# Splitting the RMS norm between two phases of a diffusion backbone: the latent half beside the last products of the phase before, the context half behind the first products of the next

## The chip, the cores and the metric

The kernel runs on one core of a Trainium2 chip. A core has TensorE (PE in the profile; PEld is its weight load), VectorE (DVE), ScalarE (ACT), GpSimd (POOL) and SyncE (SP, which here issues the loads), each with a queue of its own that is worked off in order, and sixteen DMA engines. The metric is the time of one execution on the device, in microseconds; the median of several executions is what counts.

## What is computed

Two layers over 256 latent tokens and 256 context tokens of width 1024. Each layer is a half-step FFN, a token mixer and a second half-step FFN, and each of the three begins with an RMS norm whose scale and shift come from a modulation (adaLN) that differs between latent and context tokens:

```python
def rmsnorm(x, g):
    xf = x.astype(F32)
    y = xf * lax.rsqrt(jnp.mean(xf * xf, axis=-1, keepdims=True) + EPS)
    return (y * g.astype(F32)).astype(x.dtype)

def modulate(x, shift, scale):
    return x * (1 + scale) + shift

def ffn_half_step(h, g, shift, scale, gate, w1, w3, w2):
    u = modulate(rmsnorm(h, g), shift, scale)
    return h + 0.5 * gate * ((jax.nn.silu(u @ w1) * (u @ w3)) @ w2)
...
for l in range(DEPTH):
    h = ffn_half_step(h, ...)
    hc = ffn_half_step(hc, ...)
    u = modulate(rmsnorm(h, g_mix[l]), mod[:, :, 3], mod[:, :, 4])
    uc = modulate(rmsnorm(hc, g_mix[l]), mod_c[:, :, 3], mod_c[:, :, 4])
    y, yc = token_mixer(u, uc, ...)
    h = h + mod[:, :, 5] * y
    h = ffn_half_step(h, ...)
    if not last:
        hc = hc + mod_c[:, :, 5] * yc
        hc = ffn_half_step(hc, ...)
return h
```

The mixer holds attention, a pooling branch and a gated linear attention, joined by gates and one output projection. In the last layer only the latent tokens leave the mixer, so the last FFN has no context half.

## The kernel before

**Layout.** Channels lie on the 128 partitions, tokens along the free axis: columns 0 to 255 are latent (one stream, NL = 256), 256 to 511 context. The residual `h` has eight tiles of 128 channels (k or dc = 0 to 7). All products are made in three fp32r matmuls (`mm3`, lines 218 to 220): each operand is split into a high and a low part, `whi`/`wlo` for weights, `hi`/`lo` for activations and `uhi`/`ulo` for a norm's result; high by high, high by low, low by high. A weight is loaded as `raw` (four buffers), then split by ScalarE (line 184) and VectorE (line 196). Tiles of 128x512 come from one pool of 71 slots; PSUM has eight banks, one tile each.

**The norm** (`norm`). `square` adds h*h into `acc`, tile by tile, as `h` grows (ScalarE squares, VectorE adds, line 445). Per stream, `mean` sums `acc` over partitions with a matmul of ones into `ms` (line 461; in fp32 it is two instructions), and ScalarE makes `rstd` of it with Ln and Exp. `some` then makes each of the eight k: `ut` = h * scale * rstd (VectorE, line 468), `uhi` (ScalarE), `ulo` (VectorE, line 472). Before, one call makes mean and tiles of the latent stream, then mean and tiles of the context stream, and only then the phase's first products are written down.

**The phase behind it.** The first products of a phase (`dense` with `by_stream`) go through all k of the latent columns for four units of weights, twelve matmuls per k, and then through all k of the context columns. In the mixer two of the four units are q projections and two k/v ones.

**The phase ahead of it.** The FFN ends in `down([6, 7], ...)`: the last two output columns together, latent products of column 6, then of 7, then context products of 6, of 7. Behind each of the four goes a `grow` (line 498: h += gate * products, by VectorE) and a `square`. The mixer's first layer ends in `out([6, 7], True)`: `dense` by stream, in which columns 6 and 7 alternate at each k, and the four grows behind all of it.

**The rest around it.** The modulation vectors are made beside all this, in small steps that `adas(n)` takes from a generator: a step loads 512 KB of `w_ada` and adds it up on VectorE in four instructions (`adaacc`, line 356), or on PE (line 326); now and then PE sums up and transposes (lines 373 and 380). `ada_edge` puts one piece of it, on PE, ahead of the second FFN's first products. The instructions are not issued strictly as written: a scheduler orders each queue ahead of time, by the order of writing among what it reckons to be ready.

**Where norms stand.** With two streams, and not the first of all: into the mixer of layer 0, the second FFN of layer 0, the first FFN of layer 1, the mixer of layer 1. The last FFN's has one stream.

Of the kernel before, what the change touches and what calls it, by code (L numbers as in the profile page):

```python
# [15 lines left out]
P = 128  # L16
T = 512
NL = 256
D = 1024
KD = 8  # L20
# [3 lines left out]
DEPTH = 2  # L24
# [44 lines left out]
class Unit:  # L69


    def __init__(self, hi, lo, need):
        self.hi, self.lo, self.need = hi, lo, need
# [63 lines left out]
class Net:  # L137
    def __init__(self, nc, a, cst, msk, vecs, wa2, out, pools, w):
        self.nc, self.a, self.cst_in, self.msk_in, self.out, self.w = nc, a, cst, msk, out, w
        self.vec_in, self.wa2_in = vecs, wa2  # L140
        self.one, self.slots, self.small, self.psum = pools
        self.table, self.users, self.tc, self.evac, self.net = None, [], None, None, self
        self.pairs = {}
        self.have = set()
        self.after, self.accs, self.owed, self.on_pe, self.edge = iter(()), [], 0, False, []


# [304 lines left out]
    def norm(self, l, i, n):  # L452

        nc = self.nc
        streams = [slice(s * NL, (s + 1) * NL) for s in range(n // NL)]
        u = [(self.slot(F32R, "uhi"), self.slot(F32R, "ulo")) for k in range(KD)]
        rstd = self.slot(name="rstd")

        def mean(c):
            ms = self.ps("ms")  # L460
            nc.tensor.matmul(ms[:, c], self.mean, self.acc[:, c], start=True, stop=True)
            self.rstd_from(ms[:, c], rstd[:, c])

        def some(s, c, ks):
            for k in ks:
                assert {(l, i, k // 4), (l, i + 1, k // 4)} <= self.have
                t, (hi, lo) = self.half("ut"), u[k]
                nc.vector.scalar_tensor_tensor(out=t, in0=self.h[:, k, c], scalar=self.am[l][i + 1][:, k, s:s + 1],
                                               in1=rstd[:, c], op0=ALU.mult, op1=ALU.mult)
                b = self.mod[l][:, 8 * i + k, s:s + 1]  # L470
                self.act(out=hi[:, c], in_=t, func=AF.Identity, bias=b)
                nc.vector.scalar_tensor_tensor(out=lo[:, c], in0=t, scalar=b, in1=hi[:, c].bitcast(F32),  # L472
                                               op0=ALU.add, op1=ALU.subtract)

        if l == 0 and i == 0:
            for c in streams:
                mean(c)
            yield u
            for parts in (([0], range(1, 4)), (range(4, KD),)):
                for ks in parts:  # L480
                    for s, c in enumerate(streams):
                        some(s, c, ks)
                yield
        else:
            for s, c in enumerate(streams):
                mean(c)
                some(s, c, range(KD))
            yield u

    def grow(self, ps, k, l, i, c, last):  # L490

# [8 lines left out]
            if last:  # L500
                self.square(k, s)

    def dense(self, units, x, n, by_stream=False):

        out = [self.ps() for _ in units]
        n = n if isinstance(n, list) else [n] * len(units)
        nk = len(x)
        for s in range(2 if by_stream else 1):
            for k in range(nk):
                for unit, o, m in zip(units, out, n):  # L510
                    c = slice(s * NL, (s + 1) * NL) if by_stream else slice(0, m)
                    if c.stop <= m:
                        self.mm3(o[:, c], unit.block(k), (x[k][0][:, c], x[k][1][:, c]), k == 0, k == nk - 1)
        self.w.done(*units)
        return out

# [17 lines left out]
    def ffn(self, l, which, n, final):  # L534
        nc, a = self.nc, self.a
        phase = 2 * l + which - 1
        i = 0 if which == 1 else 6
        w1, w3, w2 = (a[f"ffn{which}_{x}"][l] for x in ("w1", "w3", "w2"))

        def unit(m):  # L540
            return [self.cols(w, 0, KD, m * P) for w in (w1, w3)]

        begin = l == 0 and which == 1
        ahead = 3 if begin else 2
        norm = self.norm(l, i, n)
        if begin:
            self.adas(5)
            u = next(norm)
            self.adas(5)
            self.w.room = ROOM_0  # L550
            first = unit(0)
            next(norm)
            self.w.room = ROOM_1
            first += unit(1) + unit(2)
        else:
            self.w.room = ROOM_FFN
            first = unit(0) + unit(1)
            u = next(norm)
            self.adas(ADA["pre"][phase])
            self.ada_edge((l, which))  # L560
        gate = self.am[l][i + 2]
# [2 lines left out]
        def tail(p1, p3):  # L564
            s = self.slot(name="silu")
            self.act(out=s[:, 0:n], in_=p1[:, 0:n], func=AF.Silu)
            nc.vector.tensor_tensor(out=s[:, 0:n], in0=s[:, 0:n], in1=p3[:, 0:n], op=ALU.mult)  # L567
            g.append(self.parts(s[:, 0:n], n))

        def up(m0, m1):  # L570
            for m in range(m0, m1):
                if m == 0:
                    if begin:
                        steps = [lambda: None] * S0 + [lambda: self.adas(S1)] * (S2 - 1) + [lambda: (self.adas(10 - (S2 - 1) * S1), next(norm))]
                        o = self.dense_first(first, u, steps)
                    else:
                        o = self.dense(first, u, n, n == T)
                    for j in range(ahead):
                        tail(*o[2 * j:2 * j + 2])
                    self.ada_edge_end()  # L580
                    if begin:
                        self.w.room = ROOM_FFN
                        self.setup_rest()
                elif m >= ahead:
                    tail(*self.dense(unit(m), u, n))
                    self.adas(ADA["up"][phase])

        def down(ks, half, spans):
            us = {k: (self.cols(w2, half * HALF, 6, k * P), self.cols(w2, half * HALF + 6, 5, k * P)) for k in ks}
            o = {k: self.ps() for k in ks}  # L590
            for c in spans:
                for k in ks:
                    for f in range(HALF):
                        self.mm3(o[k][:, c], us[k][f // 6].block(f % 6), (g[f][0][:, c], g[f][1][:, c]), f == 0, f == HALF - 1)
                    self.grow(o[k], k, l, i + 2, c, half == 1)
            for k in ks:
                self.w.done(*us[k])
            if len(ks) == 1:
                self.adas(ADA["down"][phase])

        if not final:
            for half in range(2):
                up(half * HALF, (half + 1) * HALF)
                for k in range(6):
                    down([k], half, [slice(0, T)])
                if half:
                    down([6, 7], half, [slice(0, NL), slice(NL, T)])
                else:
                    down([6], half, [slice(0, T)])
                    down([7], half, [slice(0, T)])  # L610
                g.clear()
            return
        up(0, 4)
        assert {(l, 8, 0), (l, 8, 1)} <= self.have

# [12 lines left out]
        for c in range(2):  # L628
# [7 lines left out]
            self.act(out=t, in_=ps, func=AF.Copy)  # L636
            gt.append(t)
        up(4, KF)
        o = [self.ps() for _ in range(4)]

# [9 lines left out]
        us = [self.cols(w2, f, 1, 0, D) for f in range(KF - LAST, KF)]  # L650
        for i in range(4):
            for f, unit_ in enumerate(us):
                product(i, KF - LAST + f, unit_)
            j, c = divmod(i, 2)
# [7 lines left out]
    def mixer(self, l):  # L662
        a = self.a
        full = l < DEPTH - 1
        n = T if full else NL
# [20 lines left out]
        units = [self.w.get(load, 1024, cut)] + [self.cols(w_in, 0, KD, c0) for c0 in (256, 0, P)]  # L686
        if l == 0:
# [1 line left out]
            self.nc.tensor.transpose(ps[:, 0:P], self.vrow, self.ident)  # L689
            self.nc.vector.tensor_copy(self.vec[1], ps[:, 0:P])  # L690
            self.vrow = None
        u = self.u = next(self.norm(l, 3, T))
        self.adas(ADA["premix"][l])
        self.ada_edge((l, 0))
        self.inp = self.dense(units, u, [T, T, n, n], True)
        self.ada_edge_end()
        self.gq, self.gk, self.gv = [], [], []
        self.oa, self.op, self.on, self.gr, self.gates, self.pz, self.m = [], [], [], [], {}, {}, {}
# [4 lines left out]
        while chains:  # L703
            for c in list(chains):
                k = next(c, None)
# [9 lines left out]
            pass  # L715
        m = [self.m[dc] for dc in range(KD)]

        def out(dcs, by_stream):
            us = [self.cols(a["w_out"][l], 0, KD, dc * P) for dc in dcs]
            o = self.dense(us, m, n, by_stream)  # L720
            for c in ([slice(0, NL), slice(NL, T)] if by_stream else [slice(0, n)]):
                for dc, p in zip(dcs, o):
                    self.grow(p, dc, l, 5, c, True)

        self.w.room = ROOM_FFN
        self.on_pe = False
        out([0, 1, 2, 3], False)
        out([4], False)
        out([5], False)
        if full:  # L730
            out([6, 7], True)
        else:
            out([6], False)
            out([7], False)

    def chain(self, *gens):
        for g in gens:
# [642 lines left out]
```

## Time and profile before

| | us |
|---|---|
| median of three runs | 2197.16 (2190.83 to 2200.12) |
| the profiled execution | 2196.74 |
| its span, first to last instruction | 2194.6 |
| mean granted clock of TensorE in it | 0.986 |
| bytes moved from and to memory | 290.43 MB, 132 GB/s in the mean |

The span leaves out what lies around the program, 2.1 us. A row of the timeline gives start and length in us, engine, line, operation, the tile written and those read, the shape, how many such instructions follow one another, and in brackets how long the engine had stood idle and what ended that. A row of the windows gives the stretch and its length, then busy time and count for PE, PEld, DVE, ACT and POOL, PE's granted clock, the DMA engines' busy share and GB/s. A row of a group ends in busy us and mean ns of one, then the idle time before them. A row of the waits gives the total, the times and the longest, in us.

### The profile page before, as it was taken

The page shows a single profiled execution, that of the slowest core. Times are in us where ns is not written, and L with a number is a line of the kernel's source. Part 1 is how long each engine was busy: PE and PEld are TensorE (multiplying, and loading weights), DVE is VectorE, ACT ScalarE, POOL GpSimd, SP SyncE. Part 2 cuts the span into 40 slices and gives each one's busy share as a digit, 9 for nine tenths or more (in the row PEclk, how much of TensorE's full clock was granted, in tenths as well). Part 3 has the DMA queues.
Part 4 walks back from the last instruction along what each step waited for, and adds up shares of the span by engine and source line. Part 5 has one row for each costly group of instructions (what it writes and reads, how often), then busy time and mean ns, then how long its engine had stood idle before and what let it go on. Part 6 is the DMA issues. An engine that isn't in the chain of part 4 may idle for free.

```text
span 2194.6 us, 30011 instructions
## 1 busy us (share of the span) xinstructions
PE 2120.3 (97%) x11524; PEld 1752.2 (80%) x11524; DVE 1348.6 (61%) x2657; ACT 893.9 (41%) x1807; POOL 5.2 (0%) x26
## 2 busy tenths in 40 slices
PE   7999999999999999999999999999999978999999
PEld 4878788876766777888788888887888867898997
DVE  4566477665365775556565585577545698666564
ACT  5223133354344445433233343222333656565452
POOL 0000000000000000000000000000000000000000
PEclk8999999999999999999999999999999999999999
DMA  9356355433432323435464454456442324466663
GB/s 313 98 151 195 101 169 147 110 96 110 121 96 58 85 70 89 127 106 151 142 174 139 128 155 117 144 164 176 127 109 73 94 65 112 116 183 173 185 192 132
DMA packets 431070, 290.43 MB, mean 132 GB/s; under 512 B 16464, under 2 KB 386768, under 8 KB 430928
## 3 DMA queue, kind: packets, MB, share of 16 engines
q1 hardware_dynamic: 430016, 287.09, 45.5%
q8 instruction: 90, 1.47, 0.3%
q10 hardware_dynamic: 912, 1.44, 0.2%
q14 instruction: 52, 0.43, 0.1%
HBM read 287.44 MB, written 1.05 MB: 131 GB/s over the span
## 4 chain that ended last, share of the span: by engine, by line
PE 81%; DVE 8%; DMA 5%; ACT 4%; issue 2%; ACTq 0%; DVEq 0%; SPq 0%
PE ps L218 19%; PE ps L220 19%; PE ps L219 19%; DMA raw<-in_ffn_w_dram 5%; PE fill L218 4%; PE fill L220 4%; PE fill L219 4%; DVE wlo L196 2%; PE ada L326 2%; ACT whi L184 1%; PE sc L1030 1%; DVE st L1223 1%; PE av L1066 1%; PE pt L1048 1%; DVE adaacc L356 1%
## 5 line engine op out<-in xcount | busy, mean ns | idle before, releaser
L196 DVE TENSOR_TENSOR wlo<-raw,whi 128x512 fp32r<-128x512 f32 (+3 forms) x912 | 530.3, 619 | 332.3 <-ACT whi L184 324.7
L184 ACT ACTIVATE whi<-raw 128x512 fp32r<-128x512 f32 (+3 forms) x912 | 472.1, 568 | 510.4 <-DMA raw<-in_ffn_w_dram 400.0
L218 PE MATMUL ps<-uhi,whi 128*128 128x512 f32 (+1 forms) x1620 | 564.2, 350 | 7.2 <-ACT uhi L184 5.1
L219 PE MATMUL ps<-ulo,whi 128*128 128x512 f32 (+1 forms) x1620 | 562.6, 348 | 0.0
L220 PE MATMUL ps<-uhi,wlo 128*128 128x512 f32 (+1 forms) x1620 | 562.2, 348 | 0.1
L218 PEld LDWEIGHTS ps<-uhi,whi 128*128 128x128 f32 x1620 | 308.0, 191 | 58.8 <-ACT uhi L184 8.9
L220 PEld LDWEIGHTS ps<-uhi,wlo 128*128 128x128 f32 x1620 | 309.0, 191 | 39.4 <-DVE wlo L196 1.5
L219 PEld LDWEIGHTS ps<-ulo,whi 128*128 128x128 f32 x1620 | 309.5, 191 | 38.2 <-DVE ulo L472 0.6
L218 PE MATMUL ps<-hi,whi 128*128 128x512 f32 (+1 forms) x738 | 271.1, 368 | 4.0 <-DVE h L498 2.5
L220 PE MATMUL ps<-hi,wlo 128*128 128x512 f32 (+1 forms) x738 | 270.5, 367 | 0.0
L219 PE MATMUL ps<-lo,whi 128*128 128x512 f32 (+1 forms) x738 | 270.3, 366 | 0.0
L356 DVE SCALAR_TENSOR_TENSOR adaacc<-raw,csil,adaacc 128x512 f32<-128x512 f32 x350 | 243.0, 743 | 5.2 <-DMA raw<-in_w_ada_dram 5.2
L218 PE MATMUL fill<-uhi,whi 128*128 128x512 f32 (+1 forms) x576 | 204.3, 355 | 0.0
L220 PE MATMUL fill<-uhi,wlo 128*128 128x512 f32 (+1 forms) x576 | 196.5, 341 | 0.0
L219 PE MATMUL fill<-ulo,whi 128*128 128x512 f32 (+1 forms) x576 | 195.9, 340 | 0.0
L567 DVE TENSOR_TENSOR silu<-silu,ps 128x512 f32<-128x512 f32 (+1 forms) x88 | 54.3, 617 | 194.6 <-PE ps L220 111.4
L218 PEld LDWEIGHTS ps<-hi,whi 128*128 128x128 f32 x738 | 139.9, 190 | 29.4 <-DVE h L498 2.7
L219 PEld LDWEIGHTS ps<-lo,whi 128*128 128x128 f32 x738 | 140.0, 190 | 22.6 <-DVE lo L196 0.2
L220 PEld LDWEIGHTS ps<-hi,wlo 128*128 128x128 f32 x738 | 139.9, 190 | 22.4
L184 ACT ACTIVATE silu<-ps 128x512 f32<-128x512 f32 (+1 forms) x88 | 47.5, 539 | 232.3 <-PE ps L220 232.2
L218 PEld LDWEIGHTS fill<-uhi,whi 128*128 128x128 f32 x576 | 109.4, 190 | 27.1 <-issue 10.9
L219 PEld LDWEIGHTS fill<-ulo,whi 128*128 128x128 f32 x576 | 109.5, 190 | 13.6 <-issue 2.4
(265 smaller groups left out, 2182.8 us busy)
## 6 DMA issues: line engine op xcount, KB each, us to landing
raw<-in_ffn_w_dram SPq DMA_DIRECT2D x198, 512.0 KB, 4.6
raw<-in_w_ada_dram SPq DMA_DIRECT2D x128, 512.0 KB, 3.9
raw<-in_w_in_dram SPq DMA_DIRECT2D x86, 512.0 KB, 4.8
raw<-in_ffn_w_dram SPq DMA_DIRECT2D x48, 384.0 KB, 4.1
raw<-in_ffn_w_dram SPq DMA_DIRECT2D x48, 320.0 KB, 3.3
raw<-in_w_branch_dram SPq DMA_DIRECT2D x48, 256.0 KB, 2.8
ada<-in_w_ada_dram SPq DMA_DIRECT2D x32, 256.0 KB, 5.4
raw<-in_w_out_dram SPq DMA_DIRECT2D x16, 512.0 KB, 4.9
```

The lines of the kernel that those rows point to most:

```text
L184: i = self.nc.scalar.activation(**k)
L196: self.nc.vector.tensor_tensor(out=lo, in0=src, in1=f32hi, op=ALU.subtract)
L218: mm(out, wh, xh, start=start, stop=False)
L219: mm(out, wh, xl, start=False, stop=False)
L220: mm(out, wl, xh, start=False, stop=stop)
L326: nc.tensor.matmul(ps[32 * g:32 * g + 32, :], self.csil[:, k, :], r[i], start=(k < 4), stop=(k >= 4))
L356: nc.vector.scalar_tensor_tensor(out=acc[s], in0=r[i], scalar=c, in1=acc[s], op0=ALU.mult, op1=ALU.add)
L567: nc.vector.tensor_tensor(out=s[:, 0:n], in0=s[:, 0:n], in1=p3[:, 0:n], op=ALU.mult)
L1030: nc.tensor.matmul(sc[:, 0:nk], q[h][:, tt * P:(tt + 1) * P], keys[h][:, k0:T], start=True, stop=True)
L1048: nc.tensor.transpose(pt[:, (2 * x + j) * P:(2 * x + j + 1) * P], ps_[j][:, (kt + x) * P:(kt + x + 1) * P], self.ident)
L1066: nc.tensor.matmul(av[0][64 * x:64 * x + 64, s * NL:(s + 1) * NL], v[2 * s + kt][:, (h + x) * 64:(h + x) * 64 + 64], pts[x][kt // 2][:, (k ...
L1223: nc.vector.scalar_tensor_tensor(out=to, in0=st[x // 4][o, x % 4, :], scalar=dec[o, hh, x:x + 1], in1=ds, op0=ALU.mult, op1=ALU.add)
```

## The change

The norm becomes a generator with more steps: it yields behind the mean of a stream and behind its tiles. `norm_ahead` makes the next phase's norm and runs its first step, the latent mean; it is called in the phase before, behind the context products of column 6 and ahead of their grow. `norm_go`, called where the whole norm was, makes the latent tiles. `dense` takes a call, `then`, that it makes behind the latent products of k = 0 and 1: the context mean and the context tiles. The steps of `adas` and `ada_edge` that stood behind the whole norm stand between its halves now. The mixer's last two output columns are made by `out_last`, one column after the other in each stream, with a grow behind each. The last FFN's norm, with one stream, keeps its order.

```diff
         else:
             for s, c in enumerate(streams):
                 mean(c)
+                yield u
                 some(s, c, range(KD))
-            yield u
+                yield u
+
+    def norm_ahead(self, l, i):
+
+        order = [(l, i) for l in range(DEPTH) for i in (0, 3, 6)]
+        self.ahead = self.norm(*order[order.index((l, i)) + 1], T)
+        next(self.ahead)
+
+    def norm_go(self, l, i, n):
+
+        norm = self.ahead
+        if norm is None:
+            norm = self.norm(l, i, n)
+            next(norm)
+        self.ahead = None
+        u = next(norm)
+        return u, lambda: [next(norm) for _ in range(2)] if n == T else None
...
                     if c.stop <= m:
                         self.mm3(o[:, c], unit.block(k), (x[k][0][:, c], x[k][1][:, c]), k == 0, k == nk - 1)
+                if then and s == 0 and k == 1:
+                    then()
...
-            u = next(norm)
+            u, rest = self.norm_go(l, i, n)
             self.adas(ADA["pre"][phase])
             self.ada_edge((l, which))
...
-                        o = self.dense(first, u, n, n == T)
+                        o = self.dense(first, u, n, n == T, rest)
...
                         self.mm3(o[k][:, c], us[k][f // 6].block(f % 6), (g[f][0][:, c], g[f][1][:, c]), f == 0, f == HALF - 1)
+                    if c.start and k == 6:
+                        self.norm_ahead(l, i)
                     self.grow(o[k], k, l, i + 2, c, half == 1)
...
-        u = self.u = next(self.norm(l, 3, T))
+        self.u, rest = self.norm_go(l, 3, T)
         self.adas(ADA["premix"][l])
         self.ada_edge((l, 0))
-        self.inp = self.dense(units, u, [T, T, n, n], True)
+        self.inp = self.dense(units, self.u, [T, T, n, n], True, rest)
...
+        def out_last(dcs):
+
+            us = [self.cols(a["w_out"][l], 0, KD, dc * P) for dc in dcs]
+            o = [self.ps() for _ in us]
+            for c in (slice(0, NL), slice(NL, T)):
+                for dc, unit, p in zip(dcs, us, o):
+                    for k in range(KD):
+                        self.mm3(p[:, c], unit.block(k), (m[k][0][:, c], m[k][1][:, c]), k == 0, k == KD - 1)
+                    if c.start and dc == dcs[0]:
+                        self.norm_ahead(l, 3)
                     self.grow(p, dc, l, 5, c, True)
+            self.w.done(*us)
...
         if full:
-            out([6, 7], True)
+            out_last([6, 7])
```

More of the change, by code (lines that the diff above doesn't have):

```diff
@@ L486, in norm @@
                 mean(c)
+                yield u
                 some(s, c, range(KD))
-            yield u
+                yield u
[8 more added lines that the diff above has]
+            next(norm)
+        self.ahead = None
+        u = next(norm)
+        return u, lambda: [next(norm) for _ in range(2)] if n == T else None
     def grow(self, ps, k, l, i, c, last):
@@ L501, in grow, with dense @@
                 self.square(k, s)
-    def dense(self, units, x, n, by_stream=False):
+    def dense(self, units, x, n, by_stream=False, then=None):
         out = [self.ps() for _ in units]
@@ L544, in ffn @@
         ahead = 3 if begin else 2
-        norm = self.norm(l, i, n)
         if begin:
+            norm = self.norm(l, i, n)
             self.adas(5)
@@ L716, in mixer, with out @@
         m = [self.m[dc] for dc in range(KD)]
-        def out(dcs, by_stream):
+        def out(dcs):
             us = [self.cols(a["w_out"][l], 0, KD, dc * P) for dc in dcs]
-            o = self.dense(us, m, n, by_stream)
-            for c in ([slice(0, NL), slice(NL, T)] if by_stream else [slice(0, n)]):
-                for dc, p in zip(dcs, o):
+            for dc, p in zip(dcs, self.dense(us, m, n)):
+                self.grow(p, dc, l, 5, slice(0, n), True)
+        def out_last(dcs):
[7 more added lines that the diff above has]
+                        self.norm_ahead(l, 3)
                     self.grow(p, dc, l, 5, c, True)
+            self.w.done(*us)
         self.w.room = ROOM_FFN
         self.on_pe = False
-        out([0, 1, 2, 3], False)
-        out([4], False)
-        out([5], False)
+        out([0, 1, 2, 3])
+        out([4])
+        out([5])
         if full:
-            out([6, 7], True)
+            out_last([6, 7])
         else:
-            out([6], False)
-            out([7], False)
+            out([6])
+            out([7])
     def chain(self, *gens):
```

## The prediction

> **What bounds the kernel now.** I read the page's first part, then the waits of TensorE behind 404 us, then PE's own timeline at the four places that the change touches.
>
> ```profile
> span 2194.6 us, 30011 instructions
> PE 2120.3 (97%) x11524; PEld 1752.2 (80%) x11524; DVE 1348.6 (61%) x2657; ACT 893.9 (41%) x1807; POOL 5.2 (0%) x26
> ...
> PE ms L461 <- DVE acc L445: 8.7, 6, 3.4
> ```
>
> PE holds 97% of the span, so a microsecond counts only where PE stands. The wait to look at is `ms` (the matmul that sums the squares) for `acc`: six times behind 404 us, 8.7 us. One of the six, the longest (3.4), belongs to the last FFN, whose norm has one stream and isn't split by the change. The others lie at four boundaries: A into the first mixer, B into the FFN behind it, C into layer 1, D into the second mixer. PE there, one row per run of instructions:
>
> ```profile
> 419.69 0.59 PE L461 MATMUL ms<-acc,cst 128*128 128x256 f32 x2
> 421.38 0.67 PE L461 MATMUL ms<-acc,cst 128*128 128x256 f32 x2 [1.09 <-DVE acc L445]
> 423.01 0.39 PE L218 MATMUL ps<-uhi,whi 128*128 128x256 f32 x1 [0.96 <-ACT uhi L184]
> ...
> 920.82 1.05 PE L326 MATMUL ada<-raw,csil 128*32 128x512 f32 x4
> 923.04 0.67 PE L461 MATMUL ms<-acc,cst 128*128 128x256 f32 x2 [1.17 <-DVE acc L445]
> 923.90 0.67 PE L461 MATMUL ms<-acc,cst 128*128 128x256 f32 x2 [0.19 <-DVE acc L445]
> 924.50 2.22 PE L326 MATMUL ada<-raw,csil 128*32 128x512 f32 x16
> 926.65 0.39 PE L218 MATMUL ps<-uhi,whi 128*128 128x256 f32 x1
> ...
> 1300.41 0.59 PE L461 MATMUL ms<-acc,cst 128*128 128x256 f32 x2
> 1302.42 0.67 PE L461 MATMUL ms<-acc,cst 128*128 128x256 f32 x2 [1.42 <-DVE acc L445]
> 1303.02 1.06 PE L373 MATMUL ada<-adaacc,cst 128*32 128x512 f32 x8
> 1304.02 0.39 PE L218 MATMUL ps<-uhi,whi 128*128 128x256 f32 x1
> ...
> 1680.57 0.59 PE L461 MATMUL ms<-acc,cst 128*128 128x256 f32 x2
> 1682.58 0.67 PE L461 MATMUL ms<-acc,cst 128*128 128x256 f32 x2 [1.42 <-DVE acc L445]
> 1683.43 0.39 PE L218 MATMUL ps<-uhi,whi 128*128 128x256 f32 x1 [0.17 <-ACT uhi L184]
> ```
>
> At A the latent mean is issued as the old phase's products end, the context mean stands 1.09 us for its `acc`, and the first product stands 0.96 us for the latent `uhi`. Both stops come from the order: PE issues both means before any product, though the first products need the latent half alone.
>
> **The change, part by part.** *What goes.* From the first non-product to the first product: A 423.01 - 419.69 = 3.32, B 926.65 - 920.82 = 5.83, C 1304.02 - 1300.41 = 3.61, D 1683.43 - 1680.57 = 2.86; together 15.62 us. Part of it is work that stays. The means' own length:
>
> ```profile
> L461 PE MATMUL ms<-acc,cst x22: 377/380/763, 22.5 to 1993.7; 128*128 128x256 f32 x22
> ```
>
> Two instructions of 0.38 last 0.59, so they start 0.21 apart, and a pair holds PE's stream for about 0.42: 0.85 per boundary, 3.4 for four. The ada matmuls stay: at B sixteen in 926.65 - 924.50 = 2.15 and four in a quarter of it, 0.54; at C eight in 1.00. Stays 7.09, goes 15.62 - 7.09 = 8.53.
>
> *A's slow clock goes too.* PE behind A, beside PE before it:
>
> ```profile
> 423.75:427.25 3.50, 3.50 (x19) 3.50 (x19) 3.50 (x10) 2.42 (x6) 0.00 (x0) 0.52 0.00 0
> ...
> 408.00:419.60 11.60, 11.60 (x99) 11.60 (x99) 2.63 (x6) 1.25 (x3) 0.00 (x0) 1.00 0.04 11
> ```
>
> At clock 1.00 a product of 256 columns takes 11.60/99 = 0.117 us; 19 of them would take 2.23, and took 3.50: 1.27 lost at clock 0.52. I count it as gone with the two stops (2.05 us) ahead of it. The other end is that it has another cause and stays: nothing gained, 2189.1 in place of the time below, a case inside the forecast's own range. The Trainium skill ("TensorE: Matmul & The Clock Gate", section "What's actually happening") has the clock halved after an idle window of about 3.4 us that runs free of the program. By that rule alone the stops at A are too short to cool PE, which speaks for the other end; the row, 0.52 right behind them, speaks against it, and I keep the term.
>
> *What is moved: the latent half.* It now starts when the latent `acc` is complete, amid the last products. At A, on DVE and in its groups from 415 to 447 us:
>
> ```profile
> 415.82 0.48 DVE L498 SCALAR_TENSOR_TENSOR h<-ps,am,h 128x256 f32<-128x256 f32 x1 [2.50 <-PE ps L220]
> 416.85 0.42 DVE L445 TENSOR_TENSOR acc<-acc,sq 128x256 f32<-128x256 f32 x1 [0.54 <-ACT sq L184]
> 419.78 0.48 DVE L498 SCALAR_TENSOR_TENSOR h<-ps,am,h 128x256 f32<-128x256 f32 x1 [2.51 <-PE ps L220]
> 420.18 0.28 DVE L690 COPY vec<-ps 128x128 f32<-128x128 f32 x1
> 420.81 0.42 DVE L445 TENSOR_TENSOR acc<-acc,sq 128x256 f32<-128x256 f32 x1 [0.35 <-ACT sq L184]
> 421.62 1.27 DVE L468 SCALAR_TENSOR_TENSOR ut<-h,am,rstd 128x256 f32<-128x256 f32 x3 [0.39 <-ACT rstd L184]
> ...
> L468 DVE SCALAR_TENSOR_TENSOR ut<-h,am,rstd 128x256 f32<-128x256 f32 x16 | 7.2, 479 | 0.4 <-ACT rstd L184 0.4
> L472 DVE SCALAR_TENSOR_TENSOR ulo<-ut,mod,uhi 128x256 fp32r<-128x256 f32 x16 | 7.2, 479 | 0.1
> ```
>
> Column 6's context products end at 415.8, column 7's at 419.7. The mean goes between them; mean to first `ut` took 421.62 - 419.69 = 1.93 and `ut` to first product 423.01 - 421.62 = 1.39, so the first latent tile is there at 415.8 + 3.32 = 419.1, before PE asks for it at 419.7 + 0.42 = 420.1. DVE makes a k in 2 x 0.45 = 0.9 us, PE eats one in 12 x 0.117 = 1.4. Hidden by DVE's idle 2.5 us; uncovered, it costs the 3.32 - 0.85 that I count as gain at A. That this early start happens although `vec` and the grow come first in the program rests on DVE's order already being one by readiness: the copy at 420.18, written behind the `acc` of 420.81, runs ahead of it.
>
> *The context half* follows 24 latent products. At A its mean is reached at 420.1 + 24 x 0.117 = 422.9, its `acc` is ready at 420.81 + 0.42 + 0.42 = 421.7: 1.2 us to spare. Its tiles must come by 420.1 + 96 x 0.117 + 0.42 = 431.8; DVE, free of the latent half by 425 (eight at 0.9), has several us in hand. So zero; behind the waiting mean all latent products queue, so without that cover it is a PE stop.
>
> *B's products in another order.* Still 96 of them, each column's latent ones now on their own. DVE stood before the four grows:
>
> ```profile
> 912.61 1.29 DVE L196 TENSOR_TENSOR wlo<-raw,whi 128x512 fp32r<-128x512 f32 x2
> 920.57 1.27 DVE L498 SCALAR_TENSOR_TENSOR h<-ps,mod,h 128x256 f32<-128x256 f32 x3 [6.66 <-PE ps L220]
> ```
>
> The latent grows can run in those 6.66 us. New there: column 6's context products write the bank that its latent grow reads, and wait for it, with column 7's 24 latent products (2.8 us) as cover.
>
> *C is the crowded one.*
>
> ```profile
> 1297.03 2.08 DVE L356 SCALAR_TENSOR_TENSOR adaacc<-raw,csil,adaacc 128x512 f32<-128x512 f32 x3 [0.69 <-DMA raw<-in_w_ada_dram]
> 1299.03 0.48 DVE L498 SCALAR_TENSOR_TENSOR h<-ps,am,h 128x256 f32<-128x256 f32 x1
> 1299.42 0.74 DVE L356 SCALAR_TENSOR_TENSOR adaacc<-raw,csil,adaacc 128x512 f32<-128x512 f32 x1
> ```
>
> DVE is taken until 1300.1, so the latent tiles come about when PE wants them, not before. Of C's 3.61 - 0.85 - 1.00 = 1.76 I take half, leaving out 0.9; ends: nothing and all.
>
> *At nothing:* the one ada step that now stands ahead of the context half at B (PE, counted) and C (four DVE instructions of 0.74, inside the hand above; its loads keep their order on SP). The table load for silu moves with the context half, under 96 latent products. The 17 tiles for `u` and `rstd` are claimed some 4 us sooner; if they had to wait for a slot, a stop like the one below, 4.0, is my upper end, nothing the lower, and I take nothing, since column 6's weights come free as they are claimed.
>
> **Sum:** 8.53 + 1.27 - 0.9 = 8.9 us. The profiled execution took 2196.74 (span 2194.6 and 2.1 around it), 0.4 under the median 2197.16: 2196.74 - 8.9 = **2187.8**.
>
> **The rivals.** One stop shows what a bad order on DVE costs:
>
> ```profile
> 1289.70 0.75 DVE L356 SCALAR_TENSOR_TENSOR adaacc<-raw,csil,adaacc 128x512 f32<-128x512 f32 x1 [0.68 <-DMA raw<-in_w_ada_dram]
> 1290.37 0.48 DVE L498 SCALAR_TENSOR_TENSOR h<-ps,am,h 128x256 f32<-128x256 f32 x1
> ...
> 1290.91 0.58 PE L218 MATMUL ps<-hi,whi 128*128 128x256 f32 x1 [2.51 <-DVE h L498]
> ...
> 1290.90:1294.30 3.40, 3.39 (x16) 3.39 (x17) 3.40 (x7) 1.57 (x3) 0.00 (x0) 0.50 0.69 180
> ...
> 1528.21 1.12 PE L380 MATMUL ada<-cst,adaev 128*128 128x128 f32 x4 [4.06 <-ACT adaev L184]
> ...
> 1528.20:1533.30 5.10, 5.09 (x14) 4.23 (x15) 4.72 (x11) 2.11 (x4) 0.00 (x0) 0.50 0.78 239
> ```
>
> Here a grow stands in DVE's queue behind an ada step that waits for its load; PE, which must not write that bank before, loses 2.51, and then 3.39 - 16 x 0.117 = 1.5 at clock 0.50: 4.0. The grow reads the bank's latent columns and the products write its context columns, and still they wait for one another. The Trainium skill ("PSUM — Partial Sum Buffer", section "PSUM bank collisions raise a hardware error") asks for just this guard, by bank and not by address; it speaks against B's new order, and the row agrees.
>
> 1. *Slower: a stop like that at each boundary.* The latent half's `ut` and `ulo` wait in DVE's queue ahead of the context grow, and the context mean stops PE inside the latent products. It decides from 1.2 us of delay at A. Price 4 x 4.0 - 8.9 = +7.1: 2203.8. For: C's queue; against: DVE's idle stretches at A, B, D. 0.12.
> 2. *It doesn't start early:* DVE and ACT keep the latent half behind the last grows, and PE saves only the context mean's stops, some 2 to 3 us: 2194. Against: the order by readiness. 0.13.
> 3. *More:* everything behind A is put in order anew, and stops that hang on order may fall out: 4.0 at 1290.91, and 4.06 + 5.10 x 0.5 = 6.6 at 1528.21. One: 2184 or 2181; both: 2177. New ones are as possible, at those prices. 0.20.
>
> **How the numbers follow.** Forecast 0.55, its own range 2185 to 2192 (C's 0.9 either way, A's 1.27, some cooling at B to D in other executions). The range 2179 to 2200 takes in rival 2 and most of 3, and leaves out both stops gone and rival 1. A measurement tells 0.5%, 11 us, from no change: faster means below 2186, which the lower end of the forecast (0.15) and rival 3 give: 0.35. Slower means above 2208, rival 1 with more stops: 0.05. Within: 0.60.
>
> **What would show it.** Right: no idle before `ms` at the four boundaries, one latent mean amid 256-column products, clock 1.00 behind A, first `ut` at A near 417.7, first product within 0.6 us of the last old one. Wrong: idle before the context mean, a product waiting for `h` at B, or new stops before L380.

## The result and the profile after

| | median, us | runs | ratio to before, 95% interval |
|---|---|---|---|
| before | 2196.69 (2190.83 to 2200.12) | 7 | |
| after | 2207.13 (2204.51 to 2211.47) | 7 | 1.005 (1.0036 to 1.0063) |

The changed kernel is 10.4 us slower, where 8.9 us less were forecast. Its line numbers are a little higher: L184 is now L185, L196 is L197, the three products L218 to L220 are L219 to L221, the sum of squares L445 is L446, the norm's L461, L468 and L472 are L462, L469 and L473, the grow L498 is L516, `ada`'s L373 is L374. The first lines of the page, then TensorE's waits behind 404 us (total, times, longest):

```profile
span 2205.3 us, 29982 instructions
...
PE 2124.8 (96%) x11524; PEld 1759.9 (80%) x11524; DVE 1349.1 (61%) x2657; ACT 893.3 (41%) x1807; POOL 5.2 (0%) x26
```

```profile
PE ps L219 <- ACT uhi L185: 8.0, 3, 3.8
...
PE ps L220 <- DVE ulo L473: 3.9, 2, 1.9
...
PE ms L462 <- DVE acc L446: 2.8, 1, 2.8
```

The change did what it says: of the six stops of `ms` for `acc`, five are gone, and the one left is the last FFN's. But the products behind the means now wait for what the norm makes, 8.0 + 3.9 us. TensorE's timeline at A, C and D in the kernel after:

```profile
413.70 0.59 PE L462 MATMUL ms<-acc,cst 128*128 128x256 f32 x2
...
418.08 0.27 PE L711 MATMUL ps<-cst,vrow 128*128 128x128 f32 x1
422.19 1.22 PE L219 MATMUL ps<-uhi,whi 128*128 128x256 f32 x4 [3.83 <-ACT uhi L185]
...
1302.04 1.06 PE L374 MATMUL ada<-adaacc,cst 128*32 128x512 f32 x8
1304.68 0.50 PE L219 MATMUL ps<-uhi,whi 128*128 128x256 f32 x2 [1.57 <-ACT uhi L185]
1307.11 0.58 PE L220 MATMUL ps<-ulo,whi 128*128 128x256 f32 x1 [1.93 <-DVE ulo L473]
...
1678.07 0.59 PE L462 MATMUL ms<-acc,cst 128*128 128x256 f32 x2
1685.17 0.50 PE L219 MATMUL ps<-uhi,whi 128*128 128x256 f32 x2 [2.56 <-ACT uhi L185]
1687.60 0.42 PE L220 MATMUL ps<-ulo,whi 128*128 128x256 f32 x1 [1.93 <-DVE ulo L473]
```

At A the latent mean is issued at 413.70, six microseconds earlier than before, as meant, and still the first product stands 3.83 us for `uhi`. What ScalarE does in between stands in its own timeline, after first and then before:

```profile
414.33 0.47 ACT L185 ACTIVATE rstd<-ms,eps 128x256 f32<-128x256 f32 x1 [3.39 <-PE ms L462]
...
415.01 0.41 ACT L185 ACTIVATE rstd<-rstd 128x256 f32<-128x256 f32 x1
415.32 3.22 ACT L185 ACTIVATE whi<-raw 128x512 fp32r<-128x512 f32 x6
...
419.22 1.13 ACT L185 ACTIVATE whi<-raw 128x512 fp32r<-128x512 f32 x2
421.63 0.51 ACT L185 ACTIVATE uhi<-ut,mod 128x256 fp32r<-128x256 f32 x1 [1.28 <-DVE ut L469]
...
1679.38 0.41 ACT L185 ACTIVATE rstd<-rstd 128x256 f32<-128x256 f32 x1
1679.68 3.22 ACT L185 ACTIVATE whi<-raw 128x512 fp32r<-128x512 f32 x6
```

```profile
393.29 1.16 ACT L184 ACTIVATE whi<-raw 128x512 fp32r<-128x512 f32 x2 [0.18 <-DMA raw<-in_w_in_dram]
395.64 1.15 ACT L184 ACTIVATE whi<-raw 128x512 fp32r<-128x512 f32 x2 [1.19 <-DMA raw<-in_w_in_dram]
397.43 1.15 ACT L184 ACTIVATE whi<-raw 128x512 fp32r<-128x512 f32 x2 [0.63 <-DMA raw<-in_w_in_dram]
```

Before, the next phase's weights are split as they land, some 20 us ahead of A. After, eight such splits run from 415.32 to 420.35, starting in the same breath in which `rstd` is done; at D (1679.38, 1679.68) it is the same. Their second half is on VectorE, ahead of `ut`:

```profile
415.97 2.50 DVE L197 TENSOR_TENSOR wlo<-raw,whi 128x512 fp32r<-128x512 f32 x4 [0.40 <-ACT whi L185]
418.38 0.48 DVE L516 SCALAR_TENSOR_TENSOR h<-ps,am,h 128x256 f32<-128x256 f32 x1
...
421.12 0.48 DVE L469 SCALAR_TENSOR_TENSOR ut<-h,am,rstd 128x256 f32<-128x256 f32 x1
```

The idle time on VectorE that was to hold the latent tiles holds weights instead, and `ut` comes at 421.12 in place of the 417.7 forecast. The load queue of the kernel after shows how long these weights were held back:

```profile
385.97 6.06 SPq L211 DMA_DIRECT2D raw<-in_w_in_dram  x4
417.29 0.37 SPq L310 DMA_DIRECT2D raw<-in_w_ada_dram  x1
```

Four loads, as many as there are `raw` buffers, are out by 392; then nothing is issued for 25 us, until the first splits free a buffer. Before, the next load went out at 395.28.

Where the microseconds are: the start of the same TensorE instruction in two profiles, subtracted, by stretches (times of before). The two right columns belong to experiments e5 and e8 below.

| stretch | after - before | e5 - before | e8 - before |
|---|---|---|---|
| up to A (419.6) | -1.5 | -1.6 | -2.3 |
| **A** (to 447.7) | +2.3 | -2.7 | -4.5 |
| to 902.9 | +0.1 | +2.0 | +0.6 |
| **B** (to 935.7) | +0.5 | -0.8 | -0.5 |
| to 1286.7 | +0.1 | -0.3 | +0.9 |
| **C** (to 1318.5) | +4.1 | -3.0 | -3.4 |
| to 1676.5 | -4.1 | +0.3 | -0.6 |
| **D** (to 1703.7) | +4.2 | -0.5 | -2.3 |
| mixer of layer 1 (to 1840.8) | +4.9 | +3.8 | +5.6 |
| the rest | +0.1 | +0.7 | +0.4 |
| together | +10.7 | -2.1 | -6.1 |

The four boundaries lose 11.1 us in place of the gain of 8.9. The mixer's +4.9, where the change has no instruction, is read in the last section. Read in the same way, the boundaries of e2, which has nothing of the change but the early request, differ from before by at most 0.2 us each; a stretch can also move without any cause in the kernel, as A does by its clock (last section).

### The profile page after: what moved, and what is told of

It reads as the page before. It is cut to its first block, busy times and chain, and to the rows that moved or that the text cites. A ratio compares the mean times of both kernels' runs of the same rounds, so it can differ in the third digit from the quotient of the medians.

```text
span 2205.3 us, 29982 instructions
## 1 busy us (share of the span) xinstructions
PE 2124.8 (96%) x11524; PEld 1759.9 (80%) x11524; DVE 1349.1 (61%) x2657; ACT 893.3 (41%) x1807; POOL 5.2 (0%) x26
## 4 chain that ended last, share of the span: by engine, by line
PE 80%; DVE 8%; DMA 7%; ACT 3%; issue 1%; SPq 0%; ACTq 0%; DVEq 0%
PE ps L219 19%; PE ps L220 19%; PE ps L221 19%; DMA raw<-in_ffn_w_dram 5%; PE fill L219 4%; PE fill L221 4%; PE fill L220 4%; DVE wlo L197 3%; PE sc L1063 1%; ACT whi L185 1%; PE ada L327 1%; DVE st L1256 1%; DMA ada<-in_w_ada_dram 1%; PE av L1099 1%; DVE adaacc L357 1%
## 5 line engine op out<-in xcount | busy, mean ns | idle before, releaser
L197 DVE TENSOR_TENSOR wlo<-raw,whi 128x512 fp32r<-128x512 f32 (+3 forms) x912 | 530.4, 620 | 327.4 <-ACT whi L185 317.4
L185 ACT ACTIVATE whi<-raw 128x512 fp32r<-128x512 f32 (+3 forms) x912 | 471.1, 567 | 498.3 <-DMA raw<-in_ffn_w_dram 396.8
L219 PE MATMUL ps<-uhi,whi 128*128 128x512 f32 (+1 forms) x1620 | 566.2, 351 | 12.3 <-ACT uhi L185 11.9
L220 PE MATMUL ps<-ulo,whi 128*128 128x512 f32 (+1 forms) x1620 | 563.9, 349 | 3.9 <-DVE ulo L473 3.9
L221 PE MATMUL ps<-uhi,wlo 128*128 128x512 f32 (+1 forms) x1620 | 563.7, 349 | 0.1
L219 PEld LDWEIGHTS ps<-uhi,whi 128*128 128x128 f32 x1620 | 309.4, 192 | 63.1 <-ACT uhi L185 15.2
L220 PEld LDWEIGHTS ps<-ulo,whi 128*128 128x128 f32 x1620 | 310.7, 192 | 42.1 <-DVE ulo L473 4.8
L221 PEld LDWEIGHTS ps<-uhi,wlo 128*128 128x128 f32 x1620 | 310.5, 192 | 40.5 <-issue 1.7
L219 PE MATMUL ps<-hi,whi 128*128 128x512 f32 (+1 forms) x738 | 271.9, 369 | 3.7 <-DVE h L516 2.2
L221 PE MATMUL ps<-hi,wlo 128*128 128x512 f32 (+1 forms) x738 | 270.4, 366 | 0.0
L220 PE MATMUL ps<-lo,whi 128*128 128x512 f32 (+1 forms) x738 | 270.2, 366 | 0.0
L219 PE MATMUL fill<-uhi,whi 128*128 128x512 f32 (+1 forms) x576 | 204.9, 356 | 0.0
L221 PE MATMUL fill<-uhi,wlo 128*128 128x512 f32 (+1 forms) x576 | 197.1, 342 | 0.0
L220 PE MATMUL fill<-ulo,whi 128*128 128x512 f32 (+1 forms) x576 | 196.5, 341 | 0.0
L219 PEld LDWEIGHTS ps<-hi,whi 128*128 128x128 f32 x738 | 139.7, 189 | 29.2 <-DVE h L516 2.4
L220 PEld LDWEIGHTS ps<-lo,whi 128*128 128x128 f32 x738 | 139.9, 190 | 22.6 <-DVE lo L197 0.2
L221 PEld LDWEIGHTS ps<-hi,wlo 128*128 128x128 f32 x738 | 139.8, 189 | 22.5
L185 ACT ACTIVATE silu<-ps 128x512 f32<-128x512 f32 (+1 forms) x88 | 47.5, 540 | 233.5 <-PE ps L221 233.5
L219 PEld LDWEIGHTS fill<-uhi,whi 128*128 128x128 f32 x576 | 110.0, 191 | 27.1 <-issue 11.5
L220 PEld LDWEIGHTS fill<-ulo,whi 128*128 128x128 f32 x576 | 110.1, 191 | 13.7 <-issue 2.4
```

Source lines behind the costliest of these rows:

```text
L185: i = self.nc.scalar.activation(**k)
L197: self.nc.vector.tensor_tensor(out=lo, in0=src, in1=f32hi, op=ALU.subtract)
L219: mm(out, wh, xh, start=start, stop=False)
L220: mm(out, wh, xl, start=False, stop=False)
L221: mm(out, wl, xh, start=False, stop=stop)
```

## The experiments

**The theory** at the start: the early claim of 17 slots holds back the weights that are fetched ahead, because the slots run out. **Rivals**: it isn't their number but the order in which slots are handed out; or the context half behind the first products, or the new `out_last`, costs it.

**e1: claim the sixteen tiles of `u` late**, on the kernel after; `rstd` stays early.

```diff
-        u = [(self.slot(F32R, "uhi"), self.slot(F32R, "ulo")) for k in range(KD)]
+        u = []
+        claim = lambda: u.extend((self.slot(F32R, "uhi"), self.slot(F32R, "ulo")) for k in range(KD))
...
                 mean(c)
                 yield u
+                if s == 0:
+                    claim()
                 some(s, c, range(KD))
```

> The changed kernel, but the 16 tiles of the norm's result are claimed where the latent tiles are made (behind the next phase's first weights), no longer where the latent mean is written. Slots theory: the early claim takes the slots that the next phase's first weights had, so that their splits fall between the phases; with the late claim the splits are back ahead of 410 us at the first boundary, PE's waits for uhi and ulo at the four boundaries are gone, and the time is 2186 to 2191 us. Order theory (the latent half comes late because the queues keep the order of writing, whatever the slots): as the changed kernel, 2207 us.

**e2: claim early, and nothing else**, on the kernel before: `u` and `rstd` are asked for where the change asks for them, but first written in the old place.

```diff
+    def claim(self):
+
+        self.early_u = [(self.slot(F32R, "uhi"), self.slot(F32R, "ulo")) for k in range(KD)], self.slot(name="rstd")
...
+                    if c.start and k == 6:
+                        self.claim()
                     self.grow(o[k], k, l, i + 2, c, half == 1)
...
             o = self.dense(us, m, n, by_stream)
+            if by_stream:
+                self.claim()
```

> The kernel before, with nothing moved but the claim: the 16 tiles and rstd are claimed at the place where the change puts its latent mean. Slots theory: slower than before by 4 to 12 us (2201 to 2209), with the splits of the first weights between the phases at A, C and D and PE waiting for uhi there. Order theory: as before, 2196.7 us within 2.

e1 took 2213.65 us (6 runs), ratio 1.0066 (1.0042 to 1.0091), outside both forecasts, and no better than the change itself (the intervals overlap); its splits still run in one block behind `rstd`:

```profile
415.32 0.41 ACT L185 ACTIVATE rstd<-rstd 128x256 f32<-128x256 f32 x1
415.63 3.23 ACT L185 ACTIVATE whi<-raw 128x512 fp32r<-128x512 f32 x6
```

e2 took 2196.57 (12 runs), ratio 0.9992 (0.9977 to 1.0008). So neither the sixteen slots nor the early request costs anything: the first theory falls. What e1 kept from the change, and e2 didn't have, is an `rstd` that is first *written* ahead of the next phase's weights.

**e3: the context half alone** behind the first products, on the kernel before; both halves otherwise where they were.

```diff
                 some(s, c, range(KD))
-            yield u
+                yield u
...
+                if then and s == 0 and k == 1:
+                    then()
...
-        self.inp = self.dense(units, u, [T, T, n, n], True)
+        self.inp = self.dense(units, u, [T, T, n, n], True, lambda: next(norm))
```

> The kernel before, with the context half alone moved behind the first latent products; the latent half and the claim stay. Both theories: the context mean's stops go (1.1 at A, 0.2 at B, 1.4 at C, 1.4 at D), 2191 to 2194 us. If it is the context half that costs (its mean stopping PE amid the latent products): slower than 2200 us, with idle before the context mean.

2203.68 us (12 runs), ratio 1.0018 (1.0004 to 1.0032): a miss of the 2191 to 2194, no gain and if anything a small loss, though no context mean stops TensorE. Its timeline of TensorE at A:

```profile
419.32 0.60 PE L461 MATMUL ms<-acc,cst 128*128 128x256 f32 x2
422.33 0.74 PE L218 MATMUL ps<-uhi,whi 128*128 128x256 f32 x4 [2.42 <-ACT uhi L184]
```

The stop for the context mean is gone, and one stop of 2.42 for the latent `uhi` stands there instead of 1.09 + 0.96. The context mean's stop had lain inside the latent chain (mean, `rstd`, `ut`, `uhi`; 422.33 - 419.32 = 3.0 us), which nothing shortens here. So the context half is worth nothing without the latent half.

**e4: the mixer's output columns one after the other**, on the kernel before (`out_last` as in the change, without `norm_ahead`).

```diff
+        def out_last(dcs):
...
+            for c in (slice(0, NL), slice(NL, T)):
+                for dc, unit, p in zip(dcs, us, o):
+                    for k in range(KD):
+                        self.mm3(p[:, c], unit.block(k), (m[k][0][:, c], m[k][1][:, c]), k == 0, k == KD - 1)
+                    self.grow(p, dc, l, 5, c, True)
```

> The kernel before, with the mixer's last two columns made one after the other and nothing else. Grows done earlier: up to 1.4 us less at B, 2195 to 2197 us. If the shared bank stops the products (a wait for h at B): up to 4 us more, 2200 us.

2196.83 us (12 runs), ratio 0.9991 (0.9976 to 1.0006): no difference. The kernel before, shared by e1 to e4, took 2199.58 (29 runs).

**e5: `rstd` in a buffer of its own**, on the kernel after. The buffer has the size of a slot, so the pool gives one up.

```diff
-NHALF, NSLOT, ROOM_FFN, ROOM_MIX, RAWS = 4, 71, 20, 20, 4
+NHALF, NSLOT, ROOM_FFN, ROOM_MIX, RAWS = 4, 70, 20, 20, 4
...
-        rstd = self.slot(name="rstd")
+        rstd = self.small.tile([P, T], F32, tag="rstd", name="rstd", bufs=1)
```

> The changed kernel with rstd in a buffer of its own, and the pool of slots cut from 71 to 70, so that the memory is the same. Claim-order theory: slots are given out in the order in which the tiles are first used in the program; rstd, whose first use waits for the latent squares, stands ahead of the next phase's first weights and holds back their slots, and with them their splits, raw buffers and loads. With rstd out of that pool the splits are back ahead of 410 us, PE's waits for uhi at A, C and D shrink to under 0.5 us, and the time is 2186 to 2192 us. Order theory (the latent half is late whatever holds the weights): 2205 to 2210 us, as the changed kernel.

**2193.69 us** (12 runs), ratio 0.998 (0.9967 to 0.9993): faster than both kernels, though above the 2186 to 2192 forecast. ScalarE's timeline has the splits back where they land:

```profile
392.53 1.16 ACT L185 ACTIVATE whi<-raw 128x512 fp32r<-128x512 f32 x2 [1.60 <-DMA raw<-in_w_in_dram]
```

**e6 and e7: the same test on another kernel.** e6 is the kernel after with only the latent mean early: context mean and context tiles are back ahead of the first products. e7 is e6 with e5's buffer.

```diff
         u = next(norm)
-        return u, lambda: [next(norm) for _ in range(2)] if n == T else None
+        if n == T:
+            next(norm), next(norm)
+        return u, None
```

> The changed kernel with the latent mean alone early: latent tiles, context mean and context tiles stand together where the whole norm stood, rstd in the slots. Claim-order theory: the weights are held back as in the changed kernel, 2203 to 2212 us, splits behind 412 us at A. If the latent tiles or the context half are what costs: about 2197 us or less.

> As the run with the mean alone early, but rstd in its own buffer and 70 slots. Claim-order theory: splits ahead of 410 us, the latent chain begun early, PE's stop at the boundary about the context mean's alone: 2189 to 2196 us. Other theories: as the run before it.

e6 took 2209.91 us (6 runs), ratio 1.0053 (1.0035 to 1.0071), as slow as the change; its splits run in one block from 414.37, behind an `rstd` of 414.06. e7 took 2198.8 (12 runs), ratio 1.0003 (0.9988 to 1.0018): its splits are out of that block, but it misses its 2189 to 2196. TensorE stands there for the context mean, 1.49 us at A, 0.81 at B, 1.81 at C and 1.79 at D. One tile moved out of the shared pool is worth 13.4 us after the change (2207.13 to 2193.69) and 11.1 here, and an early `rstd` alone is enough to cost it. Before, shared by e5 to e7, took 2196.98 (23 runs), close to the 2196.69 beside which 2207.13 was measured.

What remained: e5 gains 3 us and not 9, and its stops for `uhi` at A and D are not under 0.5. VectorE's timeline of e5 at A, then TensorE's:

```profile
415.09 0.42 DVE L446 TENSOR_TENSOR acc<-acc,sq 128x256 f32<-128x256 f32 x1 [0.76 <-ACT sq L185]
418.23 0.48 DVE L516 SCALAR_TENSOR_TENSOR h<-ps,am,h 128x256 f32<-128x256 f32 x1 [2.72 <-PE ps L221]
418.63 0.28 DVE L712 COPY vec<-ps 128x128 f32<-128x128 f32 x1
418.83 0.48 DVE L469 SCALAR_TENSOR_TENSOR ut<-h,am,rstd 128x256 f32<-128x256 f32 x1
```

```profile
418.03 0.27 PE L711 MATMUL ps<-cst,vrow 128*128 128x128 f32 x1
419.90 0.74 PE L219 MATMUL ps<-uhi,whi 128*128 128x256 f32 x4 [1.60 <-ACT uhi L185]
```

VectorE is idle for 2.72 us with `rstd` ready, and yet `ut` runs only behind the last grow. The same kind of order can do it: `ut` shares four buffers of one tag with `sq`, and the last context `sq` is written ahead of the first `ut` in the program. In the idle stretch none of the four holds an `sq` that is still wanted: the last one was read by 415.09 + 0.42, and the next is written at 418.75, behind that grow.

**e8: `ut` in buffers of its own** on top of e5 (four of them, so two slots fewer). **e9: the two slots fewer alone. e10: e5's buffer in the kernel before.**

```diff
-NHALF, NSLOT, ROOM_FFN, ROOM_MIX, RAWS = 4, 70, 20, 20, 4
+NHALF, NSLOT, ROOM_FFN, ROOM_MIX, RAWS = 4, 68, 20, 20, 4
...
-                t, (hi, lo) = self.half("ut"), u[k]
+                t, (hi, lo) = self.small.tile([P, NL], F32, tag="ut", name="ut", bufs=4), u[k]
```

> e5 with 68 slots in place of 70 and a tag of four buffers of its own for ut, which shared the four half-width buffers with sq. Theory: buffers of a tag are handed out in the order of first use in the program, so in e5 the first ut (418.83 us at A, behind the last grow at 418.23, though rstd is ready at 415.36 and DVE idle from 415.5 to 418.2) waits for the sq of column 7's context half. With its own buffers ut runs ahead of the last grow at A and D, PE's stops there (1.60 and 1.51 us for uhi in e5) shrink below 0.5, and C's 0.70 + 0.52 shrinks too: 3 to 4 us below e5, 2188 to 2191. Rival: ut waits for something else (DVE's order, u's slots): stops as in e5, and 2193 to 2196 as the two slots fewer allow.

> Control of e8: e5 with 68 slots in place of 70 and nothing else. If the count of slots matters little, as e1 and e2 let one think, the time of e5 within 3 us (2191 to 2197) with stops of about 1.5 us for uhi at A and D. If it matters, slower than e5 by more than 3 us, and e8 has to be read against this one.

> Control of e5: the kernel before with rstd in its own buffer and 70 slots. There rstd is first written right ahead of the next phase's products, behind the weights that are fetched ahead, so its place in the order of slots holds nothing back. Theory: the time of before within 2 us. Rival: a slot for rstd costs both kernels, and e5's gain is this and not the change: 3 us or more below before.

| | median, us (12 runs each) | ratio, 95% interval |
|---|---|---|
| before (29 runs) | 2197.4 | |
| e8 | **2190.77** | 0.9964 (0.9951 to 0.9977) |
| e9 | 2193.21 | 0.998 (0.9968 to 0.9991) |
| e10 | 2197.95 | 0.9996 (0.9984 to 1.0009) |

e8 at A, VectorE and then TensorE:

```profile
414.72 1.27 DVE L469 SCALAR_TENSOR_TENSOR ut<-h,am,rstd 128x256 f32<-128x256 f32 x3
...
417.88 0.48 DVE L516 SCALAR_TENSOR_TENSOR h<-ps,am,h 128x256 f32<-128x256 f32 x1
```

```profile
417.31 0.27 PE L711 MATMUL ps<-cst,vrow 128*128 128x128 f32 x1
417.34 0.36 PE L219 MATMUL ps<-uhi,whi 128*128 128x256 f32 x1
...
1292.87 1.06 PE L374 MATMUL ada<-adaacc,cst 128*32 128x512 f32 x8
1293.87 0.38 PE L219 MATMUL ps<-uhi,whi 128*128 128x256 f32 x1
1294.52 0.39 PE L220 MATMUL ps<-ulo,whi 128*128 128x256 f32 x1 [0.26 <-DVE ulo L473]
```

Three `ut` run ahead of the last grow, and the first product follows the last old one with no stop; at C 0.26 us is left there of 3.5, and TensorE's waits behind 404 us have no row for `uhi` any more and this one alone for `ulo`. Not all is gone at C: the latent mean stands 0.70 us there for `acc`, in e5, e8 and e9 alike. So `ut` did wait for `sq`'s buffers. In the medians e8 is 2.4 us below e9, with intervals that overlap; the stops gone at A and D (1.60 and 1.51 us in e5, the same again in e9) say more than these. e9 says that two slots don't matter, e10 that e5's buffer does nothing for the kernel before: what it removes came with the change. e5, e8 and e9 are below both kernels, and e8 is the lowest: 6.6 us under before in the medians, 5 to 11 by the interval.

## Why the prediction was wrong

The forecast was 2187.8 us in a range of 2179 to 2200; the kernel took 2207.13, slower than before instead of faster. By the prediction's own steps:

- **The step that failed** is under "At nothing": "The 17 tiles for `u` and `rstd` are claimed some 4 us sooner; ... I take nothing, since column 6's weights come free as they are claimed." It asked whether the slots suffice, and they do (e1, e2, e9). It didn't ask who stands behind them in line. Asking early costs nothing (e2), writing `rstd` early does (e6), and with a buffer of its own it doesn't (e5, e7); that fits tiles which share buffers getting them in the order of their first use in the program, and e8 is a second case. `rstd`, which can't be written before the latent squares are done, now stood ahead of the next phase's weights, so these waited from 392 to 415 us with their four loads in hand. The price was bounded at one stop of 4.0; it was paid at three boundaries (+2.3, +4.1, +4.2) and the gain didn't come.
- **The early start of the latent half** failed for the same kind of reason: "rests on DVE's order already being one by readiness". `ut` was ready by its data but not by its buffer. It cost e5 the 1.6 us at A and 1.5 at D that e8 has back.
- **The sum of the stops** came out near, partly by luck. In e8, where both orders are mended, the boundaries give 4.5 + 0.5 + 3.4 + 2.3 = 10.7 us, where 8.9 were forecast: 3.3 - 0.85 + 1.27 = 3.7 at A, 2.3 at B, 0.9 at C and 2.0 at D. Of A's 4.5, 1.5 is the clock of the next point. At B two terms counted as staying grew: the sixteen ada matmuls take 2.70 us and not 2.15, and the four others stand 0.54 for their load. Of C's 3.4, 3.2 lies ahead of the means, by the same reading of starts: the stop for `h` there, priced at 4.0 with its slow clock, shrank to 0.77 at full clock (first two rows below, timeline and window of e8). That isn't shown to be the change's, since e10, without any of it, has this stop at 1.10 and full clock too. The norm's own stops then give about 3.0 + 0.5 + 0.2 + 2.3 = 6.0 us in this profile, against 7.6 forecast without the clock; the medians of e8 and before differ by 6.6.

```profile
1283.40 0.39 PE L219 MATMUL ps<-hi,whi 128*128 128x256 f32 x1 [0.77 <-DVE h L516]
```

```profile
1283.40:1287.00 3.60, 3.60 (x30) 3.60 (x31) 3.60 (x7) 1.57 (x3) 0.00 (x0) 1.00 0.65 168
...
417.40:427.40 10.00, 10.00 (x84) 9.95 (x83) 9.85 (x26) 5.41 (x13) 0.00 (x0) 1.00 0.01 2
```

- **A's slow clock**, 1.27 of the sum, is not shown to go with the stops. The last row has 1.00 behind A where before had 0.52, but so have e4 and e10, which keep A's two stops as they were; e2, with the same stops, has 0.51. In e4 and e10 A is 1.5 us shorter than before by the clock alone. The term belongs at least in part to the one execution that was profiled, which is the other end that the prediction named.
- **Moving the context half** costs nothing, as forecast: e8's context mean stops TensorE at none of the four boundaries. e3 adds what the forecast hadn't said: without the early latent half it gains nothing either.
- **The rivals.** Rival 1 came nearest in its time (2203.8) and had the sign right, and stops came at three of its four boundaries; but that is luck, for its mechanism, `ut` and `ulo` in VectorE's queue ahead of the grow, isn't what happened. Rival 2 saw the latent half stay behind the last grows, which is what e5 does at A, with 2193.69 against its 2194; that is another kernel than the one forecast. Rival 3's stop at 1528.21 did get cheaper after the change, 3.02 us and no slow clock behind it, which is 3.4 of the table's -4.1. It need not be the change's: e5 and e8 don't have it, and e10, without the change, is 1.8 us shorter at this place.

## What to carry to other kernels

Before moving the first write of a tile forward, list what stands behind it in its pool: a tile that shares buffers with prefetched weights and is itself written late blocked the weights here, though the slots would have sufficed. Give such a tile, and any that shares a tag with work of another phase, a buffer of its own, and look in the profile for a block of splits that starts just as one small tile is done, and for a load queue that is silent for as long. A stop that was removed was worth nothing where the chain behind it stayed as long (e3). And before a slow clock in one profile is counted as gain, look whether other executions of the same code have it.

## What else the runs showed of the hardware

**The same stop cools TensorE in one execution and not in another.** In the mixer of layer 1 the code is the same before and after. One stop there, in the timeline and the window behind it, before and then after:

```profile
1803.67 0.46 PE L1240 MATMUL o<-Asum,gv 128*128 128x128 f32 x2 [2.35 <-DVE Asum L1236]
```

```profile
1803.67:1808.67 5.00, 5.00 (x43) 5.00 (x44) 3.99 (x11) 3.61 (x10) 0.00 (x0) 1.00 0.01 3
```

```profile
1810.93 0.77 PE L1273 MATMUL o<-Asum,gv 128*128 128x128 f32 x2 [2.36 <-DVE Asum L1269]
```

```profile
1810.93:1815.93 5.00, 5.00 (x23) 5.00 (x24) 3.99 (x11) 3.61 (x10) 0.00 (x0) 0.50 0.02 3
```

2.35 and 2.36 us of idleness, and then a granted clock of 1.00 or 0.50: 43 matmuls in 5 us, or 23. From this stop to the instruction that starts at 1808 before, the kernel after falls 3.1 us back, most of the mixer's +4.9.

A shows the same. The stops there in e10, 1.09 and 0.96 us as before, and the window behind them:

```profile
419.76 0.67 PE L461 MATMUL ms<-acc,cst 128*128 128x256 f32 x2 [1.09 <-DVE acc L445]
...
421.39 0.74 PE L218 MATMUL ps<-uhi,whi 128*128 128x256 f32 x4 [0.96 <-ACT uhi L184]
```

```profile
422.13:425.63 3.50, 3.50 (x31) 3.50 (x31) 3.50 (x10) 2.42 (x6) 0.00 (x0) 1.00 0.00 0
```

That is 31 matmuls in 3.5 us at 1.00, where before had 19 at 0.52. e4 is as e10, e2 as before (18 at 0.51). The Trainium skill ("TensorE: Matmul & The Clock Gate", section "What's actually happening") has the clock halved after an idle window of about 3.4 us, which runs free of the program. That it runs free fits both pairs. Whether a stop must last 3.4 us is less plain: the 2.36 above was followed by the halved clock, and so were e3's 2.42 at A, with 0.6 us of the mean's work just ahead of it, and, in the profiles of before and e2 but not of e4 and e10, the 1.09 and 0.96 with the mean between them, while e5's 1.60 at the same place was not. The windows behind e3's stop and then e5's:

```profile
422.40:427.00 4.60, 4.60 (x25) 4.55 (x26) 4.60 (x13) 3.65 (x9) 0.00 (x0) 0.63 0.00 0
```

```profile
419.90:425.00 5.10, 5.10 (x41) 5.05 (x42) 5.10 (x14) 3.80 (x9) 0.00 (x0) 1.00 0.00 0
```

The mixer's +4.9 therefore says little of the change. Against the same profile of before, this stretch is 0.0 us longer in e4, +0.5 in e9, +1.2 in e1, e6 and e10, +5.0 in e3 and, by the table, +3.8 in e5 and +5.6 in e8, which are faster than before; e5 and e9 differ by two slots alone. The boundaries follow the kernel instead: e1 and e6, as slow as the change, lose 10.7 and 11.0 us at the four of them, where the change loses 11.1. How much the mixer adds to the 10.4 us between the medians stays open, since each profile is one execution.
